# Two of four gate column blocks as seven block products, with weight sums made by accumulating DMA

## The chip, the cores and the metric

The kernel runs on one core of one Trainium2 chip. The metric is the device time of one execution in microseconds, the median of several runs. A profiled execution gives the traces that are quoted; times inside it count from the start of its span.

## The reference

Two layers of a hybrid encoder trunk over x (256 tokens x 2048 channels, float32). In each layer an RMS-normed x is projected by `w_in`; four branches (A sparse attention, B retention, C gated recurrence, M attention into memory tokens) of width 512 are made from parts of it; the last four parts of the projection are four gates of width 2048, one for each branch. The end of the layer is what the change touches:

```python
h = rms_norm(x, norm_g)
u = h @ w_in                      # ..., gates: 4 x 2048 columns
...
gate_all = gates.reshape(B, S, N_BRANCH, D_MODEL)
merged = jnp.zeros_like(x)
for n, (y, z) in enumerate(((y_a, a_z), (y_b, b_z), (y_c, c_z), (y_m, m_z))):
    branch = y.reshape(B, S, W).astype(dt) * jax.nn.silu(z)
    merged = merged + jax.nn.sigmoid(gate_all[:, :, n]) * (branch @ w_branch[n])
return x + merged @ w_out
```

So for each branch n there is a gate product [256 x 2048] @ [2048 x 2048] and a small "bridge" product [256 x 512] @ [512 x 2048]. In the kernel a gate is made in four column blocks d = 0..3 of 512 columns.

## The kernel before, in words

All large products are in float32 made of three passes of the fast float32r format: both operands are split into a high part (`hi`, rounded) and a low part (`lo`, the rest), and a product is hi.hi + hi.lo + lo.hi.

**Weights.** `gemm_plan` lists, in order of use, slabs of 512 rows x 512 columns (1 MB). `load` brings a slab into a `raw` tile by one DMA on SyncE's queue (SP); there are `RAW = 4` such tiles, so four slabs are ahead. `split_weights` cuts half a slab (256 rows): ScalarE casts it into `whi`, VectorE subtracts to get `wlo`. There are `HL = 4` pairs of these, so after each half that TensorE has used, the half four further on is cut. After the second half of a slab `next_load` issues the next load into the freed tile.

**Products.** `gemms` takes one half slab after the other. For one half it issues 12 matmuls: two groups of 128 rows, two halves of the tokens (t = 0, 1), three passes. Every large matmul has a stationary [128 x 128] tile of activations and 512 moving columns of weights, and adds into a PSUM tile [128, 2, 512] from the pool `psg` (two tiles); a second pool `psb` (two tiles) serves the smaller products of the branches.

**Order of the work.** The program is written out in the order in which it is issued, engine by engine; nothing reorders it. After each half `stream.pump` counts a tick (`stream.ticks`, one tick for a full half slab) and lets the pending tasks go on: small Python generators (the branches' own work) that issue a few instructions and yield. `rest(n)` waits n ticks; a task may wait for a due time (`until`) before its last step, which splits the branch's result into hi and lo. `stream.finish(task)` forces a task to its end at once, with ticks that pass without matmuls. `fold` transposes a tile: VectorE transposes 32 x 32 blocks, then 16 small DMAs, alternately on GpSimd's queue (POOL) and SP's, move the blocks; `tick` issues at most `MOVES = 5` of them a tick. Costs that `Account` assumes only decide how many task steps are issued at a time.

**The gate stage.** For d in 0..3, for n in `BR_ORDER = (2, 0, 3, 1)` (C, A, M, B): the gate product of block d of branch n (four slabs, eight ticks), its sigmoid on ScalarE, the bridge of this block (one slab, two ticks), and on VectorE a multiply, and an add into `acc`. After four branches the sum of block d is transposed and split by the task `merged` (`mgp`, `mg0` to `mg3`). The branches' results are due at `gates_at` + 3 (C), 11 (A), 20 (M) and 30 (B) ticks, where `gates_at` is the start of the gate stage.

**The output projection.** It takes the four split sums as its rows, column blocks 0 and 1 together in `PAIR_ORDER`, then 2 and 3. Its result is added to the residual `xs`, which stays in SBUF. In the first layer the sum is also transposed, scaled and split for the next layer (`turned`).

A tile of the pool `gen` (`G`, 20 tiles of 4 KB a partition) is used by nearly everything else.

Of the kernel before, what the change touches and what calls it, by code (L numbers as in the profile page):

```python
# [33 lines left out]
    + [(O_G + n * DM + d * 512, 512) for d in range(4) for n in BR_ORDER]  # L34
# [116 lines left out]
PAIR_ORDER = ((0, 0), (0, 1), (0, 2), (1, 0), (1, 1), (1, 2), (0, 3), (1, 3))  # L151
HALVES = (slice(0, 256), slice(256, 512))
GEN, HL, RAW = 20, 4, 4
MOVES, STEPS, BANKS, WARM = 5, 2, 2, 7
# [3 lines left out]
class Stream:  # L158
    def __init__(self, account):
        self.account = account  # L160
        self.loaded = self.cut = self.used = self.ticks = self.idle = self.banks = 0
        self.owed = self.due = self.sent = 0
        self.raw, self.parts, self.tasks, self.moves, self.urgent = deque(), deque(), [], deque(), []
# [54 lines left out]

def gemm_plan(wmem, win, wbr, wout):
    p = []  # L220

    def add(src, off, n, nb=4):
        p.extend((src, off + b * 512 * n, n) for b in range(nb))

    p.extend((wmem, i * DM * 512 + b * 512 * 512, 512) for b in range(4) for i in range(2 * L))

    def pair(*at):
        p.extend((src, off + b * 512 * 512, 512) for (src, off), b in ((at[i], b) for i, b in PAIR_ORDER))

    for l in range(L):  # L230
        pair(*((win, l * DM * INW + CHUNK_AT[c]) for c in (O_CF, O_CQ)))
        for c, n in CHUNKS[2:16]:
            add(win, l * DM * INW + CHUNK_AT[c], n)
        for d in range(4):
            for n in BR_ORDER:
                add(win, l * DM * INW + CHUNK_AT[O_G + n * DM + d * 512], 512)
                add(wbr, ((l * 4 + n) * 4 + d) * W * 512, 512, 1)
        pair(*((wout, (l * 4 + c) * DM * 512) for c in range(2)))
        for c in range(2, 4):
            add(wout, (l * 4 + c) * DM * 512, 512)  # L240
    return p
# [9 lines left out]
def trunk(ctx: ExitStack, tc: tile.TileContext, x, xt, memt, ng, qkg, hg, lbl, win, wmem, wbr, wout,  # L251
          cf, out):
    nc = tc.nc
# [8 lines left out]
    sml = ctx.enter_context(tc.tile_pool(name="sml", bufs=24))  # L262
    psg = ctx.enter_context(tc.tile_pool(name="psg", bufs=2, space=bass.MemoryType.PSUM))
# [14 lines left out]
    xs = cst.tile([128, 2, DM], F32, name="xs")  # L278
# [5 lines left out]
    hgs = cst.tile([128, 2, W], F32, name="hgs")  # L284
# [6 lines left out]
    plan = gemm_plan(wmem, win, wbr, wout)  # L291
    stream = Stream(account)
# [30 lines left out]
    def split_weights():  # L323
        raw, n = stream.raw[0]
        j = stream.cut % 2
# [10 lines left out]
    def gemms(lhs, outs, n, names, tail=False, order=None, then=None):  # L336
        tiles = [psg.tile([128, 2, 512], F32, tag="pg", name=name) for name in names[:2]]
        tiles += [PB(name).rearrange("p (t n) -> p t n", t=2) for name in names[2:]]
        rows = [[ps[:, t, :] for t in range(2)] for ps in tiles]
        if tail:  # L340
            rows[0][1] = PB(names[0] + "1")[:, :512]
        nb = len(lhs)
        for o, b, j in order or [(o, b, j) for o in range(len(outs)) for b in range(nb) for j in range(2)]:
            if isinstance(lhs[b], Task):
                lhs[b] = stream.finish(lhs[b])
            ah, al = lhs[b]
            ps, (src, off) = rows[o], outs[o]
            assert (stream.used < 4) or plan[stream.used // 2] == (src, off + b * 512 * n, n)
            wh, wl = stream.parts.popleft()
# [12 lines left out]
            stream.used += 1  # L362
            stream.pump(n / 512)
            if stream.cut < 2 * len(plan):
                split_weights()
# [138 lines left out]
    def head_norm(ps, zs, g, name, until):  # L504
        v = ps.rearrange("p (a d) -> p a d", a=8)
        zg = G([128, 2, 512], name + "zg")
        ve.tensor_tensor(zg, zs, g[:, None, :].to_broadcast([128, 2, W]), op=OP.mult)
# [440 lines left out]
    def first_squares(c):  # L948
        yield from stream.rest(19 + 2 * c)
        sy.dma_start(xs[:, :, c * 512:c * 512 + 512], x[:, :, c * 512:c * 512 + 512])  # L950
        yield from stream.rest(7)
        for t in range(2):
            sq = G([128, 512], "xsq")
            ac.activation(sq, xs[:, t, c * 512:c * 512 + 512], AF.Square,
                          accum_out=ssq0[:, t * 4 + c:t * 4 + c + 1])
# [55 lines left out]
    for l in range(L):  # L1011
        sy.dma_start(hgs.rearrange("p a b -> p (a b)"), hg[l].partition_broadcast(128))

# [6 lines left out]
        def mixed(scores, v, z, g, name, until):  # L1020
            sc = yield from wait_for(box, key(scores))
            vt = yield from wait_for(box, key(v))
            zs = yield from wait_for(box, key(z))
            yield
            yield from stream.bank()
            return (yield from head_norm(mix_values(sc, vt, name), zs, g, name + "n", until))
# [22 lines left out]
        br[2] = stream.add(mixed("cs", "ci", "cz", hgs[:, 1, :], "c", gates_at + 3))  # L1049
# [8 lines left out]
        br[0] = stream.add(attend(box, [key(n) for n in ("aq", "ak", "av", "az", "ix")], "a", gates_at + 11))  # L1058
# [4 lines left out]
        br[3] = stream.add(recall(box, [key("mq"), f"mk{l}", f"mv{l}", key("mz")], "m", gates_at + 20))  # L1063
# [5 lines left out]
        br[1] = stream.add(mixed("bs", "bv", "bz", hgs[:, 0, :], "b", gates_at + 30))  # L1069
# [7 lines left out]
        mg = []  # L1077
        for d in range(4):
            acc = G([128, 2, 512], f"acc{d}")
            for i, n in enumerate(BR_ORDER):  # L1080
                pg = proj(O_G + n * DM + d * 512)
                gt = G([128, 2, 512], "gate")
                for t in range(2):
                    ac.activation(gt[:, t, :], pg[:, t, :], AF.Sigmoid, scale=rs[:, t:t + 1])
                if isinstance(br[n], Task):
                    br[n] = stream.finish(br[n])
                pb = gemm([br[n]], wbr, ((l * 4 + n) * 4 + d) * W * 512, 512, "bw")
                if i == 0:
                    ve.tensor_mul(acc, pb, gt)
                else:  # L1090
                    ve.tensor_mul(gt, pb, gt)
                    ve.tensor_tensor(acc, acc, gt, op=OP.add)
            mg.append(stream.add(merged(acc, d)))
# [12 lines left out]

        def added(c, l=l):
            def take(ps):
                for t in range(2):
                    xc = xs[:, t, c * 512:c * 512 + 512]  # L1110
                    ve.tensor_add(xc, ps[t] if isinstance(ps, list) else ps[:, t, :], xc)
                    if l == L - 1:
                        sy.dma_start(out[:, t, c * 512:c * 512 + 512], xc)
                if l + 1 < L:
                    nx.append(stream.add(turned(c, xs[:, :, c * 512:c * 512 + 512], nssq)))
            return take

        wo = [(wout, (l * 4 + c) * DM * 512) for c in range(4)]
        gemms(mg, wo[:2], 512, ["wo", "wo"], order=[(i, b, j) for i, b in PAIR_ORDER for j in range(2)], then=[added(0), added(1)])
        for c in (2, 3):  # L1120
            added(c)(gemm(mg, *wo[c], 512, "wo", tail=l == L - 1 and c == 3))
# [52 lines left out]
```

## Time and profile before

| | |
|---|---|
| median of 3 runs | 1862.95 us (1862.92 to 1863.67) |
| span of the profiled execution | 1861.4 us |
| busy: TensorE / VectorE / ScalarE / GpSimd | 1854.2 / 1154.0 / 883.6 / 247.9 us |
| moved by DMA | 381.14 MB, mean 205 GB/s |
| gate stage of the first layer | about 451 to 889 us |
| output projection of the first layer | about 889 to 976 us |

The profiled execution is one run of its own; its span is measured from its first to its last instruction, so it lies a little under the time of the runs. PE is TensorE, PEld its weight loads, DVE VectorE, ACT ScalarE, POOL GpSimd, SP SyncE; "SPq" and "POOLq" are their DMA queues. Nearly all instructions have the lines of three helpers (L127 for VectorE, ScalarE and GpSimd, L145 for TensorE, L306 for the slab loads), so groups are told apart by their tiles: `u` is a column block of the input projection, `bw` a bridge, `wo` the output projection, `whi` and `wlo` the cut weights, `raw` a slab.

### The profile page before, as it was taken

The page shows a single profiled execution, that of the slowest core. Times are in us where ns is not written, and L with a number is a line of the kernel's source. Part 1 is how long each engine was busy: PE and PEld are TensorE (multiplying, and loading weights), DVE is VectorE, ACT ScalarE, POOL GpSimd, SP SyncE. Part 2 cuts the span into 40 slices and gives each one's busy share as a digit, 9 for nine tenths or more (in the row PEclk, how much of TensorE's full clock was granted, in tenths as well). Part 3 has the DMA queues.
Part 4 walks back from the last instruction along what each step waited for, and adds up shares of the span by engine and source line. Part 5 has one row for each costly group of instructions (what it writes and reads, how often), then busy time and mean ns, then how long its engine had stood idle before and what let it go on. Part 6 is the DMA issues. An engine that isn't in the chain of part 4 may idle for free.

```text
span 1861.4 us, 23856 instructions
## 1 busy us (share of the span) xinstructions
PE 1854.2 (100%) x9076; PEld 1544.0 (83%) x9076; DVE 1154.0 (62%) x1262; ACT 883.6 (47%) x1033; POOL 247.9 (13%) x405
## 2 busy tenths in 40 slices
PE   9999999999999999999999999999999999999999
PEld 7888888888888888888888888888888888888887
DVE  5655778777655555555565577867765555555554
ACT  5654454545444444444455454454454444444442
POOL 0022023303100000000021202331310000000000
PEclk9999999999999999999999999999999999999999
DMA  8785658669555565565686565866955656566563
GB/s 328 260 257 161 238 177 222 205 199 228 170 201 196 202 195 201 188 208 195 201 232 211 168 232 174 231 208 188 225 187 185 214 186 210 189 201 200 189 207 121
DMA packets 166242, 381.14 MB, mean 205 GB/s; under 512 B 111984, under 2 KB 113264, under 8 KB 125552
## 3 DMA queue, kind: packets, MB, share of 16 engines
q1 hardware_dynamic: 153552, 367.41, 60.9%
q0 software_dynamic: 12288, 11.95, 3.6%
q8 instruction: 71, 1.16, 0.3%
q14 instruction: 43, 0.35, 0.1%
q10 hardware_dynamic: 288, 0.26, 0.0%
HBM read 353.60 MB, written 2.10 MB: 191 GB/s over the span
## 4 chain that ended last, share of the span: by engine, by line
PE 99%; DVE 0%; DMA 0%; issue 0%; ACT 0%; SPq 0%
PE u L145 73%; PE wo L145 9%; PE bw L145 9%; PE mk L145 2%; PE mv L145 2%; PE ixrp L145 0%; PE mlg L145 0%; PE mov L145 0%; PE bo L145 0%; PE co L145 0%; PE aov L145 0%; PE cl L145 0%; PE bs L145 0%; PE alg L145 0%; DMA raw<-in_wmem 0%
## 5 line engine op out<-in xcount | busy, mean ns | idle before, releaser
L127 DVE TENSOR_TENSOR wlo<-raw,whi 128x1024 fp32r<-128x1024 f32 (+2 forms) x676 | 805.5, 1194 | 660.5 <-ACT whi L127 659.7
L127 ACT CAST whi<-raw 128x1024 fp32r<-128x1024 f32 (+2 forms) x676 | 696.6, 1031 | 911.2 <-PE u L145 690.6
L127 POOL DMA_DIRECT2D mgp<-mgpi x64 | 36.9, 584 | 777.0 <-ACT whi L127 388.3
L145 PE MATMUL u<-whi,x03h 128*128 128x512 f32 (+2 forms) x256 | 98.7, 385 | 0.0
L145 PE MATMUL u<-whi,x13h 128*128 128x512 f32 (+2 forms) x256 | 98.7, 385 | 0.0
L145 PE MATMUL u<-whi,x02h 128*128 128x512 f32 (+2 forms) x256 | 98.7, 385 | 0.0
L145 PE MATMUL u<-whi,x12h 128*128 128x512 f32 (+2 forms) x256 | 98.7, 385 | 0.0
L145 PE MATMUL u<-whi,x01h 128*128 128x512 f32 (+2 forms) x256 | 98.6, 385 | 0.0
L145 PE MATMUL u<-whi,x11h 128*128 128x512 f32 (+2 forms) x256 | 98.6, 385 | 0.0
L145 PE MATMUL u<-whi,x00h 128*128 128x512 f32 (+2 forms) x256 | 98.3, 384 | 0.0
L145 PE MATMUL u<-whi,x10h 128*128 128x512 f32 (+2 forms) x256 | 98.3, 384 | 0.0
L145 PE MATMUL u<-wlo,x01h 128*128 128x512 f32 (+2 forms) x256 | 98.2, 383 | 0.0
L145 PE MATMUL u<-wlo,x11h 128*128 128x512 f32 (+2 forms) x256 | 98.2, 383 | 0.0
L145 PE MATMUL u<-wlo,x12h 128*128 128x512 f32 (+2 forms) x256 | 98.2, 383 | 0.0
L145 PE MATMUL u<-wlo,x02h 128*128 128x512 f32 (+2 forms) x256 | 98.2, 383 | 0.0
L145 PE MATMUL u<-wlo,x03h 128*128 128x512 f32 (+2 forms) x256 | 98.2, 383 | 0.0
L145 PE MATMUL u<-wlo,x13h 128*128 128x512 f32 (+2 forms) x256 | 98.2, 383 | 0.0
L145 PE MATMUL u<-whi,x03l 128*128 128x512 f32 (+2 forms) x256 | 98.2, 383 | 0.0
L145 PE MATMUL u<-whi,x13l 128*128 128x512 f32 (+2 forms) x256 | 98.2, 383 | 0.0
L145 PE MATMUL u<-wlo,x00h 128*128 128x512 f32 (+2 forms) x256 | 98.1, 383 | 0.0
L145 PE MATMUL u<-wlo,x10h 128*128 128x512 f32 (+2 forms) x256 | 98.1, 383 | 0.0
L145 PE MATMUL u<-whi,x02l 128*128 128x512 f32 (+2 forms) x256 | 98.1, 383 | 0.0
(382 smaller groups left out, 3705.3 us busy)
## 6 DMA issues: line engine op xcount, KB each, us to landing
raw<-in_win SPq DMA_DIRECT2D x240, 1024.0 KB, 4.9
raw<-in_wbr SPq DMA_DIRECT2D x32, 1024.0 KB, 4.8
raw<-in_wout SPq DMA_DIRECT2D x32, 1024.0 KB, 4.9
raw<-in_wmem SPq DMA_DIRECT2D x12, 1024.0 KB, 5.2
raw<-in_win SPq DMA_DIRECT2D x8, 656.0 KB, 4.2
raw<-in_win SPq DMA_DIRECT2D x8, 512.0 KB, 3.5
raw<-in_wmem SPq DMA_DIRECT2D x4, 512.0 KB, 7.1
xr<-in_xt SPq DMA_DIRECT2D x4, 512.0 KB, 5.8
```

Source lines behind the costliest of these rows:

```text
L127: return call(*args, **kw)
L145: return self.engine.matmul(out, w, x, **kw)
```

## The change

For branches A, M and B (`DUO = (0, 3, 1)`) the column blocks 2 and 3 of the gate are no longer made by two products. The activations are seen as a 2 x 2 block matrix (two halves of the tokens x two halves of the 2048 rows) and the weights of the two column blocks as another (two halves of the rows x two column blocks); their product is made from seven block products [128 x 1024] @ [1024 x 512] instead of eight, after the scheme of Strassen and Winograd. Blocks 0 and 1, all bridges and all of branch C stay as they were.

- Four sums of activation blocks are made once a layer (`forms`): VectorE adds and subtracts, and each is split into hi and lo (a pool `spool` of eight tiles).
- Sums of weight blocks are made by DMA: a chain of four tiles (`chains`, 256 rows each) is loaded by SP (stages 0 and 2 of `STAGES`) or added to by an accumulating DMA from GpSimd's queue (stages 1, 3, 4 and 5). After a stage has been cut, the next is issued into the same tile. The first loads are issued `AHEAD = 10` cuts ahead. Six of the seven products use these sums; one uses plain slabs.
- In `product` a half slab serves one token half only: 6 matmuls instead of 12. A half tick passes.
- Gates go branch by branch: all four blocks of C, then the groups (`two_gates`) of A, M and B. Four `acc` tiles live at the same time. The branches' results A, M and B are due at 40, 80 and 120 ticks, and at the start of the first group all are finished by `finish`.
- In a group products, halves of plain gate products and bridges alternate; both `psb` tiles hold products (`px`, `py`).
- The output projection goes through rows block by block (`SIDE_ORDER`): both column blocks with `mg0`, then both with `mg1`, and so on.
- The residual no longer stays in SBUF: it is read from DRAM ahead of the projection, and in the first layer the new one is written to a DRAM tile `x1`. The norm weights `hgs` are loaded where a branch uses them. The space that GpSimd's DMA descriptors have is set to 4096.

The core of the diff:

```diff
+DUO, AHEAD = (0, 3, 1), 10
+STAGES = ((False, 1, 3), (True, 0, 3), (False, 0, 2), (True, 0, 3), (True, 1, 3), (True, 1, 2))
...
+        for n in BR_ORDER:
+            if n not in DUO:
+                for d in range(4):
+                    gate(l, n, d)
+                    bridge(l, n, d)
+                continue
+            group = (l, n)
+            starts[len(cuts) - AHEAD] = group
+            sums(group, 0)
+            gate(l, n, 0, (0, 1))
+            sums(group, 1)
+            gate(l, n, 0, (2, 3))
+            sums(group, 2)
+            bridge(l, n, 0)
+            gate(l, n, 2, (2, 3))
+            sums(group, 3)
+            gate(l, n, 1, (0, 1))
+            sums(group, 4)
+            gate(l, n, 1, (2, 3))
+            sums(group, 5)
+            for d in range(1, 4):
+                bridge(l, n, d)
...
     def split_weights():
+        if stream.cut in starts:
+            group = starts[stream.cut]
+            chains[group] = [G([128, 2, 512], "sum") for h in range(4)]
+            for h in range(4):
+                add_block(group, 0, h)
+        if cuts[stream.cut]:
+            group, stage, h = cuts[stream.cut]
+            cut_piece(*half(512), chains[group][h])
+            if stage + 1 < len(STAGES):
+                add_block(group, stage + 1, h)
+            return
...
+    def add_block(group, stage, h):
+        adds, rows, d = STAGES[stage]
+        to = chains[group][h].rearrange("p k n -> p (k n)")
+        block = dram(win, gate_at(*group, d) + (2 * rows + h // 2) * 512 * 512 + h % 2 * 1024, 2048, 1024)
+        if adds:
+            po.dma_start(to, block, accum_op=OP.add)
+        else:
+            sy.dma_start(to, block)
...
+    def product(out, form, start=True, slabs=False):
+        for h in range(4):
+            wh, wl = stream.parts.popleft()
+            stream.used += slabs
+            for k in range(2):
+                fh, fl = form(2 * h + k)
+                for i, (a, b) in enumerate(((fh, wh), (fh, wl), (fl, wh))):
+                    te.matmul(out, a, b[:, k, :], start=start and h + k + i == 0, stop=h + k == 4 and i == 2,
+                              skip_group_check=True)
+            advance(0.5)
...
+            product(px[:, 0, :], summed(2))
+            ac.copy(qs[:, 0, :], px[:, 0, :])
+            pg = half_gate(0, (0, 1))
+            product(px[:, 1, :], summed(3))
+            ac.copy(q7, px[:, 1, :])
+            gt = gated(half_gate(0, (2, 3), pg)[0])
+            product(py[:, 0, :], plain(0, 0))
+            ac.copy(qs[:, 1, :], py[:, 0, :])
+            bridge(n, 0, gt)
+            product(py[:, 0, :], plain(2, 0), start=False, slabs=True)
+            sigmoid(first, 0, py[:, 0, :])
+            product(px[:, 0, :], summed(0))
+            pg = half_gate(1, (0, 1))
+            product(py[:, 1, :], summed(1))
+            ve.tensor_add(us[:, 0, :], py[:, 1, :], qs[:, 1, :])
...
+            gt = gated(half_gate(1, (2, 3), pg)[0])
+            product(px[:, 1, :], plain(2, 1), start=False)
+            ve.tensor_add(first[:, 1, :], px[:, 1, :], us[:, 0, :])
+            sigmoid(first, 1, first[:, 1, :])
+            bridge(n, 1, gt)
+            bridge(n, 2, first)
+            bridge(n, 3, second)
...
+        for n in BR_ORDER:
+            if n in DUO:
+                for m in BR_ORDER:
+                    if isinstance(br[m], Task) and n == DUO[0]:
+                        br[m] = stream.finish(br[m])
+                if isinstance(ready, Task):
+                    ready = stream.finish(ready)
+                two_gates(n)
+            else:
+                for d in range(4):
+                    bridge(n, d, gated(proj(O_G + n * DM + d * 512)))
...
         def added(c, l=l):
+            xc = residual(c)
+
             def take(ps):
                 for t in range(2):
-                    xc = xs[:, t, c * 512:c * 512 + 512]
-                    ve.tensor_add(xc, ps[t] if isinstance(ps, list) else ps[:, t, :], xc)
-                    if l == L - 1:
-                        sy.dma_start(out[:, t, c * 512:c * 512 + 512], xc)
+                    ve.tensor_add(xc[:, t, :], ps[t] if isinstance(ps, list) else ps[:, t, :], xc[:, t, :])
+                    sy.dma_start((out if l == L - 1 else x1)[:, t, c * 512:c * 512 + 512], xc[:, t, :])
```

More of the change, by code (lines that the diff above doesn't have):

```diff
@@ L33 @@
     + [(O_MQ, 512), (O_MZ, 512), (O_BQ, 512), (O_BK, 512), (O_BV, 512), (O_BZ, 512)]
-    + [(O_G + n * DM + d * 512, 512) for d in range(4) for n in BR_ORDER]
+    + [(O_G + n * DM + d * 512, 512) for n in BR_ORDER for d in range(4)]
 )
@@ L160, in __init__ @@
         self.account = account
-        self.loaded = self.cut = self.used = self.ticks = self.idle = self.banks = 0
+        self.loaded = self.cut = self.halves = self.used = self.ticks = self.idle = self.banks = 0
         self.owed = self.due = self.sent = 0
@@ L216, in finish, with gate_at, slab, add @@
         return t.value
+def gate_at(l, n, d):
+    return l * DM * INW + CHUNK_AT[O_G + n * DM + d * 512]
 def gemm_plan(wmem, win, wbr, wout):
[L220 to L228, printed above, removed]
+    p, cuts, starts = [], [], {}
+    def slab(*entry):
+        p.append(entry)
+        cuts.extend([None, None])
+    def add(src, off, n, blocks=range(4)):
+        for b in blocks:
+            slab(src, off + b * 512 * n, n)
+    def pair(order, *at):
+        for i, b in order:
+            src, off = at[i]
+            slab(src, off + b * 512 * 512, 512)
+    def gate(l, n, d, blocks=range(4)):
+        add(win, gate_at(l, n, d), 512, blocks)
+    def bridge(l, n, d):
+        add(wbr, ((l * 4 + n) * 4 + d) * W * 512, 512, range(1))
+    def sums(group, stage):
+        cuts.extend((group, stage, h) for h in range(4))
+    for b in range(4):
+        for i in range(2 * L):
+            slab(wmem, i * DM * 512 + b * 512 * 512, 512)
@@ L230, in gemm_plan @@
     for l in range(L):
-        pair(*((win, l * DM * INW + CHUNK_AT[c]) for c in (O_CF, O_CQ)))
+        pair(PAIR_ORDER, *((win, l * DM * INW + CHUNK_AT[c]) for c in (O_CF, O_CQ)))
         for c, n in CHUNKS[2:16]:
             add(win, l * DM * INW + CHUNK_AT[c], n)
[L234 to L238, printed above, removed]
+        for n in BR_ORDER:
[20 more added lines that the diff above has]
+                bridge(l, n, d)
@@ L239, in gemm_plan @@
+        pair(SIDE_ORDER, *((wout, (l * 4 + c) * DM * 512) for c in range(2)))
         for c in range(2, 4):
             add(wout, (l * 4 + c) * DM * 512, 512)
-    return p
+    return p, cuts, starts
 def wait_for(box, key):
@@ L289, in trunk @@
     ve.memset(ones, 1.0)
-    plan = gemm_plan(wmem, win, wbr, wout)
-    stream = Stream(account)
+    x1 = kept.tile([128, 2, DM], F32, name="x1")
+    plan, cuts, starts = gemm_plan(wmem, win, wbr, wout)
+    stream, chains = Stream(account), {}
     def load(pieces=((0, 4),)):
@@ L323, in split_weights @@
     def split_weights():
+        if stream.cut in starts:
[9 more added lines that the diff above has]
+            return
         raw, n = stream.raw[0]
-        j = stream.cut % 2
+        j = stream.halves % 2
+        stream.halves += 1
         hi, lo = half(n)
@@ L334, in next_load, with advance, gemms @@
             load()
-    def gemms(lhs, outs, n, names, tail=False, order=None, then=None):
-        tiles = [psg.tile([128, 2, 512], F32, tag="pg", name=name) for name in names[:2]]
+    def advance(part):
+        stream.pump(part)
+        if stream.cut < len(cuts):
+            split_weights()
+    def gemms(lhs, outs, n, names, tail=False, order=None, then=None, tiles=None):
+        tiles = tiles or [psg.tile([128, 2, 512], F32, tag="pg", name=name) for name in names[:2]]
         tiles += [PB(name).rearrange("p (t n) -> p t n", t=2) for name in names[2:]]
@@ L362, in gemms @@
             stream.used += 1
-            stream.pump(n / 512)
-            if stream.cut < 2 * len(plan):
-                split_weights()
+            advance(n / 512)
             if then and b == nb - 1 and j:
@@ L1068, in trunk @@
         stream.add(keep(key("bs"), retain()))
[L1069 removed]
+        br[1] = stream.add(mixed("bs", "bv", "bz", 0, "b", gates_at + 120))
         box[key("bv")] = evac(proj(O_BV), rs, "bv")
@@ L1075, in merged, with forms, held, total @@
             return split(u, gen, "g", f"mg{d}")
[L1077 to L1093, printed above, removed]
+        def forms():
+            made = []
+            def held(b, t):
+                return [u[:, :, 128 * t:128 * t + 128].bitcast(F32) for u in xh[b]]
+            def total(name, first, *signed):
+                out = first or G([128, 8, 128], name)
+                for p in range(2):
+                    to = out[:, 4 * p:4 * p + 4, :]
+                    terms = [(u, sign) for sign, b, t in signed for u in held(b + p, t)]
+                    if first is None:
+                        (h, _), (g, sign), *_ = terms[::2]
+                        (ve.tensor_add if sign > 0 else ve.tensor_sub)(to, h, g)
+                        terms = terms[1::2]
+                    for u, sign in terms:
+                        (ve.tensor_add if sign > 0 else ve.tensor_sub)(to, to, u)
+                    yield
+                hi, lo = (spool.tile([128, 8, 128], F32R, tag="s", name=name + e) for e in "hl")
+                ac.copy(hi, out)
+                yield
+                ve.tensor_sub(lo, out, hi.bitcast(F32))
+                made.append((hi, lo))
+                return out
+            s1 = yield from total("s1", None, (1, 0, 1), (-1, 2, 1))
+            s2 = yield from total("s2", s1, (-1, 0, 0))
+            yield from total("r4", s2, (1, 2, 0))
+            yield from total("s3", None, (1, 0, 0), (-1, 0, 1))
+            return made
@@ new lines, in trunk, with merged, sigmoid, gated @@
+        acc, mg = [None] * 4, []
+        def merged(d):
+            u = yield from transposed(acc[d], "mgp")
+            return split(u, gen, "g", f"mg{d}")
+        def sigmoid(gt, t, src, rs=rs):
+            ac.activation(gt[:, t, :], src, AF.Sigmoid, scale=rs[:, t:t + 1])
+        def gated(pg):
+            gt = G([128, 2, 512], "gate")
+            for t in range(2):
+                sigmoid(gt, t, pg[:, t, :])
+            return gt
+        def bridge(n, d, gt, l=l):
+            if isinstance(br[n], Task):
+                br[n] = stream.finish(br[n])
+            pb = gemm([br[n]], wbr, ((l * 4 + n) * 4 + d) * W * 512, 512, "bw")
+            if acc[d] is None:
+                acc[d] = G([128, 2, 512], f"acc{d}")
+                ve.tensor_mul(acc[d], pb, gt)
+            else:
+                ve.tensor_mul(gt, pb, gt)
+                ve.tensor_tensor(acc[d], acc[d], gt, op=OP.add)
+            if n == BR_ORDER[-1]:
+                mg.append(stream.add(merged(d)))
@@ new lines, in plain, with form, summed, two_gates @@
+        def plain(b, t):
+            def form(k):
+                return [u[:, k % 4, 128 * t:128 * t + 128] for u in xh[b + k // 4]]
+            return form
+        def summed(i):
+            def form(k):
+                return [u[:, k, :] for u in ready[i]]
+            return form
+        def two_gates(n, l=l):
+            stream.banks = BANKS
+            px, py = (PB(name).rearrange("p (t n) -> p t n", t=2) for name in ("px", "py"))
+            qs, us = G([128, 2, 512], "qs"), G([128, 2, 512], "us")
+            q7 = G([128, 512], "q7")
+            first, second = G([128, 2, 512], "gate"), G([128, 2, 512], "gate")
+            def half_gate(d, blocks, tiles=None):
+                order = [(0, b, j) for b in blocks for j in range(2)]
+                return gemms(xh, [(win, gate_at(l, n, d))], 512, ["u"], order=order, tiles=tiles)
+            product(px[:, 0, :], summed(2))
[13 more added lines that the diff above has]
+            ve.tensor_add(us[:, 0, :], py[:, 1, :], qs[:, 1, :])
+            ve.tensor_add(us[:, 1, :], us[:, 0, :], q7)
+            ve.tensor_sub(qs[:, 0, :], qs[:, 0, :], us[:, 0, :])
+            ve.tensor_add(second[:, 0, :], px[:, 0, :], qs[:, 0, :])
+            sigmoid(second, 0, second[:, 0, :])
+            ve.tensor_sub(second[:, 1, :], px[:, 0, :], us[:, 1, :])
+            sigmoid(second, 1, second[:, 1, :])
+            gt = gated(half_gate(1, (2, 3), pg)[0])
[5 more added lines that the diff above has]
+            bridge(n, 3, second)
+            stream.banks = 0
@@ L1105, in trunk, with residual @@
         nx = []
+        def residual(c, l=l):
+            xc = G([128, 2, 512], "xc")
+            sy.dma_start(xc, (x1 if l else x)[:, :, c * 512:c * 512 + 512])
+            return xc
         def added(c, l=l):
+            xc = residual(c)
             def take(ps):
                 for t in range(2):
[L1110 to L1113 removed]
+                    ve.tensor_add(xc[:, t, :], ps[t] if isinstance(ps, list) else ps[:, t, :], xc[:, t, :])
+                    sy.dma_start((out if l == L - 1 else x1)[:, t, c * 512:c * 512 + 512], xc[:, t, :])
                 if l + 1 < L:
[L1115 removed]
+                    nx.append(stream.add(turned(c, xc, nssq)))
             return take
         wo = [(wout, (l * 4 + c) * DM * 512) for c in range(4)]
[L1119 removed]
+        gemms(mg, wo[:2], 512, ["wo", "wo"], order=[(i, b, j) for i, b in SIDE_ORDER for j in range(2)], then=[added(0), added(1)])
+        later = [added(c) for c in (2, 3)]
         for c in (2, 3):
[L1121 removed]
+            later[c - 2](gemm(mg, *wo[c], 512, "wo", tail=l == L - 1 and c == 3))
         if l + 1 < L:
```

38 lines of the change are left out of this document (21 added, 17 removed).

## The prediction

> **What bounds the kernel now.** I read the page first (busy time, slices, chain), then the chain in order of time, then the busy time by stretches, then the groups of the gate stage, then single instructions around one bridge.
>
> ```profile
> span 1861.4 us, 23856 instructions
> PE 1854.2 (100%) x9076; PEld 1544.0 (83%) x9076; DVE 1154.0 (62%) x1262; ACT 883.6 (47%) x1033; POOL 247.9 (13%) x405
> PEclk9999999999999999999999999999999999999999
> PE 99%; DVE 0%; DMA 0%; issue 0%; ACT 0%; SPq 0%
> 557.66 5.44 PE bw L145 x24
> 563.11 21.76 PE u L145 x96
> ```
>
> TensorE is busy for 1854.2 of 1861.4 us and is 99% of the chain; the granted clock is full in all slices. In the chain a gate product follows its bridge without a gap: 96 matmuls in 21.76 us, so 226.7 ns for one [128x128]x[128x512] matmul, 12 of them (one half slab) in 2.72 us. Only fewer matmuls can make this kernel faster, and a wait of TensorE costs its full length.
>
> ```profile
> core 0: us, PE busy (x) PEld busy (x) DVE busy (x) ACT busy (x) POOL busy (x), PEclk, DMA share, GB/s
> 8.00:24.00 16.00, 16.00 (x72) 13.22 (x71) 10.52 (x13) 9.45 (x12) 0.00 (x0) 1.00 1.02 400
> 451.00:560.00 109.00, 109.00 (x511) 91.36 (x510) 67.74 (x61) 51.27 (x55) 7.22 (x9) 1.00 0.57 188
> 670.00:780.00 110.00, 110.00 (x487) 91.09 (x486) 60.09 (x50) 48.07 (x50) 4.61 (x8) 1.00 0.58 198
> L127 DVE TENSOR_TENSOR wlo<-raw,whi 128x1024 fp32r<-128x1024 f32 x122 | 149.0, 1223 | 151.4 <-ACT whi L127 151.4
> L127 ACT CAST whi<-raw 128x1024 fp32r<-128x1024 f32 x121 | 127.7, 1055 | 183.5 <-PE u L145 154.8 <-PE bw L145 23.7 <-DMA mgp<-mgpi 5.0
> L127 ACT ACTIVATE gate<-u,rs0r 128x512 f32<-128x512 f32 x24 | 15.1, 680 | 0.0
> L127 DVE TENSOR_TENSOR acc<-acc,gate 128x1024 f32<-128x1024 f32 x9 | 11.0, 1224 | 0.3
> ```
>
> The columns of the first rows are the stretch, its length and each engine's busy time; the others give busy time and mean ns. In the gate stage DVE works 55% and ACT 44% of the time, DMA 58%. Sixteen DMA engines are full (share 1.02) at 400 GB/s.
>
> **Part 1: matmuls removed.** In a group (one of three branches, per layer) column blocks 2 and 3 took 2 x 96 matmuls. Now they are seven products of 4 half slabs x 6 matmuls, 168. So 24 x 226.7 ns = 5.44 us go, in 6 groups 32.6 us. All new matmuls have the old shape, two of three use the same stationary tile in a row as before, so I keep 226.7 ns. Blocks 0 and 1, the bridges and the fourth branch keep their matmuls. A group then lasts 456 x 226.7 ns = 103.4 us.
>
> **Part 2: cuts.** A half slab is cut by one cast (1055 ns) and one subtraction (1223 ns). Blocks 2 and 3 needed 16 cuts, the seven products need 28. A group has 52 cuts: DVE 63.6 us, plus four bridges' multiply and add (1.22 us each, 9.8), plus six half-size operations at half of that (3.7), so 77 of 103 us; ACT 55 plus eight sigmoids and three copies of 0.68, 62 of 103. On average both fit. Locally a product half lasts 6 x 226.7 = 1.36 us instead of 2.72, and each half that TensorE leaves frees the buffers (four) for the cut of the half four further on. What DVE does at the end of a bridge is then the question:
>
> ```profile
> 889.34 0.39 PE L145 MATMUL wo<-whi,mg0h 128*128 128x512 f32 x1
> 889.54 1.05 ACT L127 CAST whi<-raw 128x1024 fp32r<-128x1024 f32 x1 [1.67 <-PE bw L145]
> 890.63 1.23 DVE L127 TENSOR_TENSOR wlo<-raw,whi 128x1024 fp32r<-128x1024 f32 x1 [1.50 <-ACT whi L127]
> 891.77 1.22 DVE L127 TENSOR_TENSOR gate<-bw,gate 128x1024 f32<-128x1024 f32 x1
> 893.02 1.22 DVE L127 TENSOR_TENSOR acc<-acc,gate 128x1024 f32<-128x1024 f32 x1
> 894.28 1.25 DVE L127 STREAM_TRANSPOSE mgpi<-acc 128x1024 f32<-128x1024 f32 x1
> 895.45 2.32 DVE L127 TENSOR_TENSOR wlo<-raw,whi 128x1024 fp32r<-128x1024 f32 x2
> ```
>
> The bridge's last matmul is followed by the next product at T = 889.34. Subtraction, multiply and add hold DVE until T+4.9, and two subtractions back to back take 1.16 us each. Where a product follows the bridge, the half behind that product is needed at T+5.44, and its subtraction is queued behind the add: it ends at T+6.2. The first matmul of a half needs only the cast, the second the low part, so TensorE stands for 6.2 - 5.44 - 0.23 = about 0.55 us. This happens twice in a group (first product after the previous branch's last bridge; product after the bridge of block 0). The other joins have room: a cut takes 0.2 + 1.05 + 1.22 = about 2.5 us, against 4.08 us for three product halves. Bounds: nothing, if the add is late elsewhere, to 1.2 us if the neighbouring subtraction also slips. I take 0.55, the working from the rows above.
>
> **Part 3: branch results finished together.** The splits of branches 3 and 1 (a cast and a subtraction each) used to stand alone between gates:
>
> ```profile
> L127 ACT CAST mh<-my x2: 1052/1052/1053, 507.0 to 1388.1; 128x1024 fp32r<-128x1024 f32 x2
> L127 DVE TENSOR_TENSOR ml<-my,mh x2: 1218/1218/1218, 508.3 to 1389.3; 128x1024 fp32r<-128x1024 f32 x2
> L127 ACT CAST bnh<-bnpt x2: 1052/1052/1053, 534.2 to 1415.3; 128x1024 fp32r<-128x1024 f32 x2
> ```
>
> Their new due times (80 and 120 ticks) lie behind the first group's start at tick 40, where the code finishes them by force, right after the bridge's add. Two more subtractions (2 x 1.16) then stand before the same cut: the first group's first wait is 0.55 + 2.3 = 2.85 us. Branch 0's split comes in the last pump ahead of the add and costs nothing. If the splits were earlier the cost is 0, if all three are late 4.0; I take 2.85. Per layer: 2.85 + 0.55 in the first group, 2 x 1.1 in the others, 5.6 us; two layers 11.2.
>
> **Part 4: the sums of activations.** Twenty half-size additions (estimate 0.61 each, half of the add's row) and four cast/subtract pairs, 17 us of DVE and 4.2 of ACT per layer, run inside the fourth branch's 108.8 us. There DVE is busy 67.74 of 109 us, so it has room, and the longest step (three additions, 1.8 us) is shorter than the 3 x 2.72 - 2.5 = 5.7 us that a cut has there. Nothing. Without that cover it would be up to 17 us a layer.
>
> **Part 5: sums of weights by DMA.** Per group 16 accumulating transfers of 512 KB on POOL's queue and 8 plain ones on SP's, beside 14 slabs. Plain bytes: 14 x 1.049 + 8 x 0.524 = 18.9 MB, at 400 GB/s 47.2 us. An accumulating DMA has no row. Bounds for what it holds all engines: a plain load at 400 GB/s, 1.31 us, or POOL's queue now:
>
> ```profile
> q1 hardware_dynamic: 153552, 367.41, 60.9%
> q0 software_dynamic: 12288, 11.95, 3.6%
> raw<-in_win SPq DMA_DIRECT2D x240, 1024.0 KB, 4.9
> raw<-in_win SPq DMA_DIRECT2D x8, 512.0 KB, 3.5
> mgp<-mgpi POOLq DMA_DIRECT2D x64, 32.0 KB, 5.0
> DMA to landing us min/median/max: 2.5/4.9/11.0
> L127 POOL DMA_DIRECT2D mgp<-mgpi x64: 584/584/593, 569.8 to 1781.2; - x64
> SPq L306 <- DVE wlo L127: 290.0, 61, 5.5
> ```
>
> 11.95 MB took 3.6% of 1861.4 us, 178 GB/s, so 2.94 us for 512 KB. The group's DMA time is 68 to 94 us of 103.4: it fits at both ends, so no wait, and I lean to the upper one, as that row is of the same queue. Time to land: a sum's next use is 12.2 us (third to fourth stage) to 20.4 us after the cut that frees it, and at the shortest join TensorE leaves 5.7 us more. Cut 2.5 + issue 0.6 + landing between 3.5 and 11.0 (the longest of a slab) is 6.6 to 14.1 us, under 17.9. Cost 0 on the path. If landing took over 14.8 us, each further us would cost one us at up to four joins a group. A wait on a cut now stands in POOL's queue; behind it are only later sums and, in the last group, the eight moves of block 0's result, needed over 30 us later. SP waits already for a cut before its slabs (290.0 us in 61 waits between 560 and 889) at no cost.
>
> The Trainium skill (DMA: Bandwidth & Descriptors, Rules for kernel authors) says that an accumulating DMA reads its destination and writes it later. No run here shows one yet. Worked out from it as an estimate, two reads per write make 2.62 us of engine time, 89 us per group; the sum would stay as it is.
>
> **Part 6: the end of a layer.** Blocks 1 to 3 of the merged result now all come in the last 16 us before the output projection; its order takes block 0 for four halves first. Block 1's bridge ends 21.8 us before its first use. How long the way takes is seen on today's last block, whose bridge ends at 889.34:
>
> ```profile
> 896.10 4.61 POOL L127 DMA_DIRECT2D mgp<-mgpi  x8 [103.47 <-ACT whi L127]
> 898.17 2.40 SPq L418 DMA_DIRECT2D mgp<-mgpi  x3
> 903.14 3.74 SPq L418 DMA_DIRECT2D mgp<-mgpi  x5
> 914.98 1.05 ACT L127 CAST mg3h<-mgp 128x1024 fp32r<-128x1024 f32 x1
> 916.25 1.22 DVE L127 TENSOR_TENSOR mg3l<-mgp,mg3h 128x1024 fp32r<-128x1024 f32 x1
> DMA to landing us min/median/max: 1.8/5.1/8.4
> ```
>
> The last moves leave at T+17.5 (903.14 + 3.74) and land 5.1 us later, T+22.6; the cast ends at about T+23.3 to 23.7 and the low part at T+24.5, needed for the third matmul (0.45 us after the first). Against 21.8 that is a wait of about 2.3 us; bounds 0 (moves sent earlier by the forced finish) and 5. Two layers: 4.6. The residual in DRAM adds 8 loads of 512 KB and 8 stores on SP; a store waits for an addition behind the projection while four slabs (21.8 us) are ahead, so nothing. The norm weight's load moves into the branch with a six-tick rest, 16 us against a landing of about 5: nothing.
>
> **The sum.** 32.6 - 11.2 - 4.6 = 16.8 us. The profiled span falls from 1861.4 to 1844.6. The median of the runs is 1862.95, 1.55 above the span; I keep that distance: 1846.
>
> **The rivals.** (a) Everything hidden: DVE has idle time in each product, and if the add or the moves come a little earlier the small waits go. Gain 32.6, time 1830. For it: 77 of 103 us of DVE; against it the queue order at the bridge.
>
> (b) Slower: an accumulating transfer holds the engines much longer than the rows of plain ones. Place: the cast of a sum at each product. It decides from (108.8 - 47.2) / 16 = 3.85 us each; from there the group lasts longer than today. At 4.4 us, 1.5 times the q0 bound, a group takes 117.6 us, 6 x 8.8 = 53 us more than now: 1916. For it: no trace here has such a transfer, and even the q0 bound fills 91% of the time; against it both bounds fit and the prefetch is deep.
>
> (c) No change: DVE's subtractions stretch while POOL writes descriptors. At 1.45 us instead of 1.16 a product's four take 0.36 us longer than its matmuls, in 42 products 15 us more of waits: about 1861 to 1862. Against it: subtractions beside POOL's moves at 896 to 900 keep 1.16 to 1.23 us. That the change removes fewer matmuls than it says I exclude by the count.
>
> **How the numbers follow.** Forecast 0.50 (own range 1836 to 1857), (a) 0.20, (c) 0.08, (b) 0.22. The range runs from 1829, just under (a), to 1878, which takes in (c) and the mild quarter of (b), and leaves out under 0.2. About 0.2%, 3.7 us, is what can be told from no change: faster 0.70, same 0.08, slower 0.22.
>
> **What would show it.** TensorE's count falls by 144, to 8932 of 9076; gaps of about half a us at the first half slab after the first product of each group and after the product behind block 0's bridge, put down to DVE; about 3 us at the first group of each layer; one or two us in the projection, put down to the cast of block 1. DMA share in the groups between 0.65 and 0.95. I am wrong if casts wait for the accumulating DMA, if the DMA share reads 1.0, or if DVE's mean subtraction is over 1.35 us.

## The result, and the profile after

The changed kernel takes 1879.6 us (median of four runs, 1877.7 to 1887.7) against 1862.9: a ratio of 1.0098 (95% interval 1.0078 to 1.0118). It is 16.7 us slower where 16.9 us of gain were forecast. The profiled execution took 1877.66 us, its span 1875.9, 14.5 more than before.

From the page of the changed kernel: the span, busy times, the clock by slices, the chain, and the rows of GpSimd's queue and of the sums.

```profile
span 1875.9 us, 24297 instructions
PE 1833.8 (98%) x8932; PEld 1517.4 (81%) x8932; DVE 1285.7 (69%) x1418; ACT 968.2 (52%) x1131; POOL 331.4 (18%) x501
...
PEclk9999999999999999999899999999999999999989
...
q0 software_dynamic: 26112, 62.29, 18.0%
...
PE 78%; DMA 7%; issue 7%; DVE 4%; ACT 2%; POOL 1%; SPq 0%; DVEq 0%; POOLq 0%; ACTq 0%
...
L127 DVE TENSOR_TENSOR wlo<-sum,whi 128x1024 fp32r<-128x1024 f32 x144 | 173.6, 1222 | 143.0 <-ACT whi L127 143.0
...
sum<-in_win POOLq DMA_DIRECT2D x96, 512.0 KB, 7.7
```

TensorE has lost its 144 matmuls, yet it is only 78% of the chain, where it was 99%: something else than matmuls sets the time in places. Two slices, at the two output projections, no longer have the full clock. TensorE's waits name the place at once (total, times, longest):

```profile
PE wo L145 <- ACT mg1h L127: 23.3, 2, 12.0
PE u L145 <- DVE wlo L127: 3.6, 6, 1.3
PE px L145 <- DVE wlo L127: 2.5, 7, 0.9
PE py L145 <- DVE wlo L127: 2.2, 3, 0.8
...
PE py L145 <- ACT whi L127: 1.0, 2, 0.8
```

By stretches (the columns as in the prediction: stretch, length, each engine's busy time, granted clock, DMA share, GB/s), about the three groups of the first layer and its projection:

```profile
562.00:668.00 106.00, 102.65 (x448) 83.47 (x447) 73.57 (x66) 61.23 (x66) 12.71 (x15) 1.00 0.89 255
668.00:775.00 107.00, 106.47 (x468) 87.22 (x467) 76.70 (x69) 60.84 (x64) 14.91 (x18) 1.00 0.92 257
775.00:883.00 108.00, 105.79 (x462) 86.01 (x461) 78.28 (x70) 60.69 (x64) 20.53 (x28) 1.00 0.89 239
883.00:986.00 103.00, 90.60 (x389) 73.48 (x388) 58.51 (x58) 42.10 (x52) 24.25 (x43) 0.95 0.79 226
```

From their first matmul to the next one's, the groups last 108.2, 104.8 and 107.0 us, where 103.4 are matmuls. The projection lasts from 883.47 to 985.62 us (first `wo` matmul to the next layer's first), 102.15 us; before it lasted from 889.34 to 976.38, 87.04. So 15.1 us are lost there, and 15.3 in the second layer. With 32.6 us of matmuls saved, 9.9 and 6.3 us lost in the groups of the two layers and 0.6 ahead of the gates, the span comes to 1861.4 - 32.6 + 9.9 + 6.3 + 15.1 + 15.3 + 0.6 = 1876.0, against 1875.9.

TensorE's own timeline at the wait (start, duration; the bracket is the idle time before):

```profile
894.12 0.39 PE L145 MATMUL wo<-whi,mg0l 128*128 128x512 f32 x1
905.84 0.80 PE L145 MATMUL wo<-whi,mg1h 128*128 128x512 f32 x1 [11.33 <-ACT mg1h L127]
906.43 0.63 PE L145 MATMUL wo<-wlo,mg1h 128*128 128x512 f32 x1
907.10 0.80 PE L145 MATMUL wo<-whi,mg1l 128*128 128x512 f32 x1
...
909.39 0.40 PE L145 MATMUL wo<-wlo,mg1h 128*128 128x512 f32 x1
909.63 0.40 PE L145 MATMUL wo<-whi,mg1l 128*128 128x512 f32 x1
```

The wait adds 11.5 us between two starts. The matmuls behind it run at half pace: eight take 905.84 to 909.63, 3.79 us instead of 1.81. The wait thus costs 2.0 us more than its length. Two smaller waits (0.53 for `mg2l`, 0.83 for a weight cut), each with 0.11 us more at the matmul behind it, bring this to 15.0 of the 15.1. The changed kernel's chain up to the cast that TensorE waited for (start, length, what):

```profile
883.60 3.81 DMA mgp<-mgpi
...
887.53 0.61 SPq L1292
...
888.19 9.17 DMA xc<-in_x
...
897.38 0.58 SPq L496
...
898.01 0.66 SPq L496
...
899.49 5.24 DMA mgp<-mgpi
...
904.74 1.05 ACT mg1h L127
...
905.84 1.22 PE wo L145 x2
```

What SyncE's queue issued in that time, and then GpSimd's (L349 slab loads, L1292 residual, L496 moves):

```profile
875.27 12.03 SPq L349 DMA_DIRECT2D raw<-in_wout  x3
887.53 1.71 SPq L1292 DMA_DIRECT2D xc<-in_x  x2
889.30 3.69 SPq L496 DMA_DIRECT2D mgp<-mgpi  x5
893.08 0.75 SPq L349 DMA_DIRECT2D raw<-in_wout  x1
895.64 4.67 SPq L496 DMA_DIRECT2D mgp<-mgpi  x5
```

```profile
879.49 4.69 POOL L127 DMA_DIRECT2D mgp<-mgpi  x8 [26.39 <-ACT whi L127]
```

The bridge of block 1 ends at T = 872.6. GpSimd's eight moves of that block leave from 879.49 on. SyncE's eight stand behind slab loads, which end at 887.3, and behind the two loads of the residual; five leave from 889.30 on, the last three after another slab load and after a residual load of 9.17 us, for whose landing SyncE waited. The eighth has left by 898.7, T + 26.1; the chain names the move behind it, which left by 899.5, T + 26.9. The cast starts at 904.74.

### The profile page after: what moved, and what is told of

Its sections match the earlier page's. It is cut to its first block, busy times and chain, and to the rows that moved or that the text cites. A ratio compares the mean times of both kernels' runs of the same rounds, so it can differ in the third digit from the quotient of the medians.

```text
span 1875.9 us, 24297 instructions
## 1 busy us (share of the span) xinstructions
PE 1833.8 (98%) x8932; PEld 1517.4 (81%) x8932; DVE 1285.7 (69%) x1418; ACT 968.2 (52%) x1131; POOL 331.4 (18%) x501
## 3 DMA queue, kind: packets, MB, share of 16 engines
q0 software_dynamic: 26112, 62.29, 18.0%
## 4 chain that ended last, share of the span: by engine, by line
PE 78%; DMA 7%; issue 7%; DVE 4%; ACT 2%; POOL 1%; SPq 0%; DVEq 0%; POOLq 0%; ACTq 0%
PE u L145 53%; PE bw L145 7%; PE wo L145 7%; DMA sum<-in_win 3%; DVE wlo L127 3%; PE px L145 3%; PE mk L145 2%; PE py L145 2%; PE mv L145 2%; ACT whi L127 2%; DMA mgp<-mgpi 1%; POOL sum L127 1%; DMA xp<-xpi 1%; DVE gate L127 1%; DMA xc<-x 1%
## 5 line engine op out<-in xcount | busy, mean ns | idle before, releaser
L127 DVE TENSOR_TENSOR wlo<-raw,whi 128x1024 fp32r<-128x1024 f32 (+3 forms) x604 | 708.5, 1188 | 372.7 <-ACT whi L127 367.9
L127 ACT CAST whi<-raw 128x1024 fp32r<-128x1024 f32 (+3 forms) x604 | 615.2, 1027 | 592.2 <-PE u L145 372.5
L127 DVE TENSOR_TENSOR wlo<-sum,whi 128x1024 fp32r<-128x1024 f32 x144 | 173.6, 1222 | 143.0 <-ACT whi L127 143.0
L127 ACT CAST whi<-sum 128x1024 fp32r<-128x1024 f32 x144 | 150.4, 1053 | 182.2 <-PE u L145 111.8
L127 POOL DMA_DIRECT2D sum<-in_win x96 | 83.5, 869 | 601.6 <-DVE wlo L127 596.1
L145 PE MATMUL u<-whi,x02h 128*128 128x512 f32 (+2 forms) x208 | 80.0, 385 | 0.0
L145 PE MATMUL u<-whi,x12h 128*128 128x512 f32 (+2 forms) x208 | 80.0, 385 | 0.0
L145 PE MATMUL u<-whi,x13h 128*128 128x512 f32 (+2 forms) x208 | 79.9, 384 | 0.0
L145 PE MATMUL u<-whi,x03h 128*128 128x512 f32 (+2 forms) x208 | 79.9, 384 | 0.0
L145 PE MATMUL u<-whi,x00l 128*128 128x512 f32 (+2 forms) x208 | 79.5, 382 | 0.0
```

The source lines that it names most:

```text
L127: return call(*args, **kw)
L145: return self.engine.matmul(out, w, x, **kw)
```

## The experiments

Each edit is made on the changed kernel. The kernel before, run beside them, took 1862.9 to 1863.1 us. Theory A says throughout that the loss lies in the late moves of the merged blocks (Part 6). The rivals put it on the new order, on the DMA sums, or on DMA load as such.

**All groups off (`e_none`).**

```diff
-DUO, AHEAD = (0, 3, 1), 10
+DUO, AHEAD = (), 10
...
-        ready = stream.add(forms())
```

> No branch in DUO and no sums of activations: gates branch by branch with plain products, residual in DRAM, SIDE_ORDER, the rest of the change. Theory A: without the group's three bridges in a row blocks 1 to 3 come 27 us apart, so there is no wait; the time is that of the kernel before, 1862 to 1865. Theory C: at least 10 us over it. Theory B says as A here.

1863.5 us, ratio 1.0003 (0.9994 to 1.0013). Residual in DRAM and the projection's new order cost nothing by themselves; everything comes with the groups.

**Merged blocks sent at once (`e_now`).** The tasks of blocks 1 to 3 are stepped right behind the bridge's add, and all 16 moves are issued there.

```diff
                 mg.append(stream.add(merged(d)))
+                if d:
+                    send_now(mg[-1])
+        def send_now(t):
+            t.step()
+            t.step()
+            while stream.moves:
+                stream.sent += 1
+                stream.moves.popleft()(stream.sent)
```

> The two first steps of the last branch's tasks (blocks 1 to 3) are issued right behind each bridge's add, and their 16 moves at once, not five a tick. Theory A (the moves of block 1 of the merged sum are issued too late, behind the residual's loads in SP's order): the wait of 11.5 and 12.2 us at mg1 goes, with the slow clock behind it, 15 us a layer; the time is 1848 to 1854. Theory B (the DMA engines are too full in the groups, the moves land late wherever they are issued): the wait stays over 8 us, 1870 to 1880. Theory C (the new order and the residual in DRAM cost by themselves): 1875 to 1880.

1846.1 us, 0.9921 (0.9899 to 0.9943), a little under the expected span of numbers. SyncE's queue in this kernel, and its projection, from the first `wo` matmul to the next layer's first, in the view by stretches:

```profile
874.38 6.43 SPq L496 DMA_DIRECT2D mgp<-mgpi  x8
880.91 0.55 SPq L349 DMA_DIRECT2D raw<-in_wout  x1
881.56 6.42 SPq L496 DMA_DIRECT2D mgp<-mgpi  x8
```

```profile
878.88:966.13 87.25, 87.25 (x386) 72.02 (x384) 57.91 (x58) 41.62 (x51) 23.88 (x42) 1.00 0.94 265
```

The eight moves now leave by 880.8, before the slab load; the projection takes 87.25 us at full clock (87.04 before), with a DMA share of 0.94, where the changed kernel had 0.79. So neither DMA load nor the order of the projection delays it. The lateness of these moves costs 33.5 us, about twice what the change lost.

**What makes the moves late.** Four edits each take away a part.

`e_hurry`: from the last bridges on, tasks go on although `Account` takes VectorE to be late; still five moves a tick.

```diff
-            if self.due < 1 or self.account.late() > LATE:
+            if self.due < 1 or self.account.late() > (1e9 if self.hurry else LATE):
...
-            if self.account.at["te"] >= t.ready:
+            if self.hurry or self.account.at["te"] >= t.ready:
```

> Between the last branch's bridge 1 and the end of the first two column blocks of the projection the tasks are not held back by the assumed lateness of VectorE (LATE) or by their ready time; the moves still go five a tick. Theory A, if this holding back is what puts the moves behind the residual's loads: the wait at mg1 falls from 12 to 2 to 6 us, time 1853 to 1864. If the order in SP's queue comes from something else: 1875 to 1880.

1869.0 us, 1.0033 (1.0023 to 1.0044): 10.6 us of the 33.5 are back, with waits of 7.7 and 5.9 us left, more than was expected. Block 1's first five moves of SyncE now leave from 878.12 on; the last three still leave behind a slab load and both residual loads, from 885.51 on. Held-back tasks are a part of the cause, not all of it.

`e_later`: the two residual loads go out ten ticks into the projection.

```diff
-            xc = residual(c)
+            def fetch():
+                yield from stream.rest(10 if c < 2 else 1)
+                return residual(c)
+            fetched = stream.add(fetch())
             def take(ps):
+                xc = stream.finish(fetched)
```

> The residual's first two loads are issued ten ticks into the projection instead of just ahead of it. Theory A with the residual's loads as the cause of the lateness (a move waits until a load of 9 us has landed): the wait at mg1 falls by about 5 us a layer, time about 1866. If the moves are late by their own order in the program: 1874 to 1880, the wait over 9 us.

1873.4 us, 1.0056 (1.0036 to 1.0077), from two runs of 1870.9 and 1875.9. This lies between the two expectations. The waits fall from 11.5 and 12.2 to 7.9 and 7.1 us, but a wait of 2.0 us for a weight cut appears later in the projection. So the residual loads are 3.6 and 5.1 us of the waits.

`e_step`: `send_now` without its loop, so the tasks are early but the moves leave five a tick. `e_flush`: the tasks stay late, but each merged block sends its 16 moves at once.

```diff
         stream.moves.extend([moved] * 16)
+        while name == "mgp" and stream.moves:
+            stream.sent += 1
+            stream.moves.popleft()(stream.sent)
```

> The tasks of the last branch's merged blocks 1 to 3 are stepped twice right behind the bridge's add (transposed, moves put in the list), but the moves leave five a tick as in the changed kernel, between the slab loads of SP. Theory A (the tasks are held back by the assumed lateness of VectorE, and that alone makes the moves late): block 1's 16 moves leave within four ticks, 11 us, land 5 us later, cast and low part end before the 21.8 us are over: wait at mg1 0 to 2 us, 1846 to 1850 us. Theory B (the moves are late because only five leave a tick and SP's share then stands behind slab loads that wait for a tile): wait at mg1 3 to 8 us a layer, as with the hurried tasks, with half clock behind it, 1854 to 1868 us.

> The tasks run as late as in the changed kernel, but when a merged block has been transposed all its 16 moves are issued at once. Theory A (held-back tasks): the transposition of block 1 at T+5 stays, SP's eight moves stand behind slab loads issued before them, up to 887 us in the changed kernel, and land by about 898: wait at mg1 4 to 7 us, 1857 to 1867 us. Theory B (five a tick): SP's eight moves leave together with POOL's, by T+12, wait at mg1 0 to 2 us, 1846 to 1850 us.

`e_step`: 1856.3 us, 0.9962 (0.9949 to 0.9974). The wait for the cast of `mg1` is gone, as theory A says, but the time lies in theory B's range, because the next block is late instead (TensorE's waits):

```profile
PE wo L145 <- ACT mg2h L127: 2.9, 2, 1.9
...
PE wo L145 <- DVE mg2l L127: 0.9, 2, 0.5
```

With half clock behind these waits the two projections take 5.8 and 3.9 us more than in `e_now`.

`e_flush`: 1861.2 us, 0.9990 (0.9980 to 0.9999). There is no wait for `mg1` either, as theory B says, and against theory A's 4 to 7 us: block 1's moves of SyncE leave from 883.55 on. The time stays in theory A's range, though, for another reason. Here block 0's moves, too, are sent at once, in the middle of the last group. From its chain and from ScalarE's timeline:

```profile
834.77 10.79 DMA sum<-in_win
...
845.84 3.50 DMA mgp<-mgpi
...
849.64 1.05 ACT mg0h L127
...
850.72 1.22 DVE mg0l L127
```

```profile
849.64 1.04 ACT L127 CAST mg0h<-mgp 128x1024 fp32r<-128x1024 f32 x1 [6.41 <-DMA mgp<-mgpi]
850.59 2.94 ACT L127 CAST whi<-raw 128x1024 fp32r<-128x1024 f32 x3
```

A move waited in GpSimd's queue until an accumulating DMA had landed, the cast of `mg0` stood for it at the head of ScalarE's queue, and three weight cuts behind it came late: TensorE stood 3.4 us, and its matmuls ran at half pace behind it. Up to the first projection this kernel loses 6.6 of the 12.4 us by which its span exceeds that of `e_now`; I did not trace the rest. So the wait at `mg1` needs both: either early tasks or moves sent at once remove it, and of these versions only both together (blocks 1 to 3 alone) leave no wait in the projection.

**All moves on GpSimd's queue (`e_pool`).**

```diff
-            move((po, sy)[i % 2], *left.pop())
+            move(po if name == "mgp" else (po, sy)[i % 2], *left.pop())
```

> As the changed kernel, tasks as late in the program as there, but all 16 moves of each block of the merged sum go on POOL's queue, none on SP's. Theory A in its narrow form (what makes block 1 late is the place of its eight SP moves behind the waits of slab and residual loads): the wait at mg1 falls from 12 to 0 to 3 us, since POOL needs 16 x 0.58 = 9.3 us from 877.7 + 1.2 and a landing of 5 to 6; time 1846 to 1853. If the late place in the program holds for POOL as well, or the engines are what is slow: wait over 6 us, 1865 or more.

1874.6 us, 1.0065 (1.0050 to 1.0080), a miss for theory A's narrow form. The time lies in the other range, but not for its reason: the waits at `mg1` fall to 4.8 and 3.3 us, and the same trap as in `e_flush` opens instead. TensorE's waits, and ScalarE's timeline:

```profile
PE px L145 <- ACT whi L127: 9.1, 2, 5.1
PE wo L145 <- ACT mg1h L127: 7.8, 2, 4.7
```

```profile
862.64 1.04 ACT L127 CAST mg0h<-mgp 128x1024 fp32r<-128x1024 f32 x1 [8.36 <-DMA mgp<-mgpi]
863.59 1.99 ACT L127 CAST whi<-sum 128x1024 fp32r<-128x1024 f32 x2
```

**Plain loads instead of the sums (`e_now_plain`)**, on `e_now`:

```diff
-            po.dma_start(to, block, accum_op=OP.add)
+            po.dma_start(to, block)
```

This kernel leaves out the additions: a tile holds the last block loaded.

> With the moves sent at once, and the 16 accumulating DMAs of a group made plain loads on the same queue; the sums of weights then hold only the last block loaded. If reading the destination is what an accumulating DMA costs: POOL's loads land in 5 to 6 us instead of 7.7, the DMA share in the groups falls from 0.9 to under 0.8, the waits of casts for sums go, time 1841 to 1844. If the queue or the descriptors are the cost: landing, share and time as before, 1845 to 1847.

1842.0 us, 0.9887 (0.9867 to 0.9907), as expected; the loads land even faster than that. The same 62.29 MB on GpSimd's queue, beside the 18.4% and 7.3 us to landing that `e_now` has; rows of the page, then the first group by stretch:

```profile
q0 software_dynamic: 26112, 62.29, 11.8%
...
sum<-in_win POOLq DMA_DIRECT2D x96, 512.0 KB, 4.7
```

```profile
562.00:668.00 106.00, 104.18 (x458) 85.26 (x457) 76.10 (x68) 61.76 (x66) 8.46 (x16) 1.00 0.73 257
```

The DMA share of a group falls from 0.89 to 0.73, and the waits for late sums (0.4 to 1.2 us each in `e_now`) are gone. Accumulating costs 4.2 us of span between the two profiled executions (1843.9 to 1839.7). The medians differ as much (1846.1 and 1842.0), but the two kernels were timed on different chips and their intervals overlap at the ends, so that the waits went is surer than the size.

**Two groups (`e_two`)**: `DUO = (0, 3)`.

> DUO = (0, 3): branches A and M in groups, the last branch B with four plain gate products; nothing else changed. Four of six savings of 5.44 us are left, 21.8. Theory A: bridges of the last branch lie 27 us apart, no wait at the projection; the groups cost about 4 us a layer, time 1847 to 1851. If the loss lay in the groups themselves and not at the projection: 1863 or more.

1855.9 us, 0.9963 (0.9951 to 0.9975): a gain, but smaller than expected. The profiled execution (1859.1) has no wait for a merged block. It has 5.2 us of late sums, and behind two pairs of them the clock falls to half for 3.4 us; the window at the first:

```profile
637.00:641.00 4.00, 3.70 (x11) 2.93 (x12) 4.00 (x5) 2.87 (x3) 0.86 (x1) 0.68 1.06 209
```

With what the matmuls behind its waits lose, about 1 us of its loss has no place.

**Earlier due times (`e_now_early`)**, on `e_now`: 11, 24 and 36 ticks instead of 40, 80 and 120.

> With the moves sent at once, and the results of branches A, M and B due at 11, 24 and 36 ticks, so that no split stands between the add and the first cut of the first group. If the 1.43 us wait at the first group is the two splits in VectorE's queue: it becomes 0.43 as at the other groups, the time falls by about 2 us to 1844. If it is something else: 1.43 stays, 1846.

1844.2 us (1843.7 to 1844.8), 0.9898 (0.9881 to 0.9914). The wait of 1.43 us at each layer's first group is gone; the span falls only from 1843.9 to 1843.0, as other small waits moved. Of the versions with true sums this is the fastest, and it beats both kernels. That it beats `e_now` is not settled: the two were timed on different chips, and their intervals overlap.

## Why the prediction was wrong, by its own steps

**Part 6 failed, and it alone turned the sign.** It put the end of a layer at 2.3 us, bounds 0 to 5; it measured 15.1 and 15.3. The step that failed is "how long the way takes is seen on today's last block". Last moves at T + 17.5 were taken over to block 1; they left at T + 26 to T + 27. Before, the last block's 16 moves were the only ones of a merged block there. Now three blocks in 16 us send 48 moves, five a tick, by tasks that are also held back, into a SyncE queue in which two residual loads (priced "nothing") and waiting slab loads stand between them. The prediction counted SyncE's new loads by what they cost TensorE, and not by what they hold up in their queue. And a long wait brought 2 us of half clock with it, which no row of before could show; it was not priced.

**Part 1 was right**: 144 matmuls fewer, at an unchanged pace (0.227 us between starts), 32.6 us.

**Part 2 was right in place and size**: at each product behind a bridge the low part of the first half slab is late by 0.43 to 0.44 us, and the matmul behind it starts another 0.11 late: 0.54 together, against 0.55.

**Part 3 was mis-sized**: 1.44 us at the first group instead of 2.85; `e_now_early` shows that the late splits caused it.

**Part 4 (sums of activations at nothing)**: no wait is put down to them.

**Part 5: cost 0 on the path was wrong by a little.** The engine time is (18.0 - 3.6)% of 1875.9 us over 96, about 2.8 us a transfer, inside the bounds of 1.31 to 2.94. The estimate of 2.62, worked out from what the Trainium skill says (DMA: Bandwidth & Descriptors, Rules for kernel authors), is near it. But in a DMA share of 0.89 to 0.92 these transfers land after 5.3 to 16.2 us, not 11 at most, so some sums come too late: 4.1 us of waits in the first layer's groups, 1.6 in the second's. Of the first layer's 9.9 us the waits are 8.1, and the 0.11 us behind each of them 1.4 more; 0.4 stay without a place.

**The rivals.** (b), engines held by accumulating DMA, does not decide: 2.8 us is under its 3.85, and the groups of both layers last 104.5 to 108.2 us, not 117. (c) is excluded: the subtraction keeps 1222 ns. The slower case came by a mechanism that stood in the forecast as a small term, not as a rival with its own price.

With the late moves mended, `e_now` gives the predicted 1846. That is no proof of every term: the 4.6 us of Part 6 and half of Part 3 are not there, and the late sums, priced at nothing, take their place. That the number comes out is in part luck.

## What to carry to other kernels

When work is bunched at a stage's end, write out every queue that its results pass, in issue order, with each load and each wait ahead of them; a transfer of 5 us that stands behind loads waiting for buffers is late by their wait, however free the engines are. Look also at what stands behind an instruction that may wait for such a transfer: moving the merged blocks to another queue moved the wait into ScalarE's weight cuts. And price a short transfer's path from the queue that it will stand in, not from the same transfer in a quiet stage.

## What the runs showed of the hardware

**Half clock after a wait.** The mean granted clock was 0.51 from 899 to 905 us in the changed kernel, while TensorE stood, and matmuls ran at half pace for 3.8 us after it. The page TensorE: Matmul & The Clock Gate of the Trainium skill (Part 1: The HAM clock gate) says that an idle window of about 3.4 us halves the clock, and a busy one releases it. The waits of 11 us agree. In `e_two` two waits of about 1 us, one right after the other, were enough (0.68 in the window above), and in `e_step` waits of 1.17 and 0.69 us (clock 0.50 from 907.3 to 910.6 us), all shorter than that window. A pair of 0.93 and 1.03 us in the changed kernel (in the first group's row above, clock 1.00) and one of 1.55 and 1.03 in `e_now_early` (1.00 from 843 to 849 us) left it full. So the length of the waits alone does not decide, and what does is open.

**Accumulating DMA.** 512 KB added by DMA took about 2.8 us of all engines, a plain load on the same queue about 1.6 ((11.8 - 3.6)% of 1839.7 us over 96). GpSimd took 862 ns to issue one, 527 ns for a plain one.
